# Hybrid encoder trunk on one core: gate projections woven apart from their branches, C's keys moved ahead of B's queries, and the last two feature tiles taken one by one

## The chip, the cores and the metric

The kernel runs on one core of one Trainium2 chip. Time is device time in microseconds (us) of that core. The core has TensorE (matrix products, PE in the profile, with its weight loads as PEld), VectorE (DVE), ScalarE (ACT), GpSimd (POOL) and SyncE (SP), which issues most transfers.

## The reference

An encoder of two layers (DEPTH = 2) works on 272 tokens: 16 learned meta tokens and 256 tokens on a grid of 4 rows by 64 columns, each with 1024 features. A layer is

```
h = h + 1/2 * SwiGLU1(RMSNorm(h))
n = RMSNorm(h)
h = h + ( sum_b sigmoid(gate_b(n)) * (mixer_b(n) @ w_branch[b]) ) @ w_out
h = h + 1/2 * SwiGLU2(RMSNorm(h))
```

SwiGLU goes through 2816 features. The three mixers b are attentions with 8 query heads of 64 features, fed by one projection of n: A has 2 key heads, a window of 128 positions, rotary positions and a sink logit for each head; B has 8 key heads, a neighbourhood of 4 rows by 16 columns and a learned bias; C has 2 key heads, is dense, and normalises each head of q and k before its rotary positions. The gates are 3 x 1024 columns of the same projection. After the last layer comes RMSNorm of all tokens, and the meta tokens are dropped. All data are float32.

## The kernel before, in words

**Layout.** The features of h stand on the partitions, eight tiles of 128 features by 272 tokens (256 where the meta tokens are no longer needed, in layer 1 from the queries on). A product in full precision is made of three products of rounded parts: `unit` (L218) loads a block of weights, 128 x 1024, into `raw`, casts it into `hi` on ScalarE (L250) and subtracts for `lo` on VectorE (L251), in the mixer for every third plain unit on GpSimd (`lo_engine`, L213). There are four buffers each of raw, hi and lo. `mm` (L284) goes over the feature tiles k and for each over two output tiles m, three matmuls each (L295 to L297). A projection of 256 columns is two units and 48 matmuls; a branch product has half of that.

**Order.** The program is written as a sequence, and a scheduler of the framework orders each engine's instructions ahead of time, by dependences, free buffers and the place in the program as priority. So the program's order sets preferences; what an engine then runs is a fixed queue. Accumulators (`acc`) have two buffers, score and transpose banks (`s`) three.

**The mixer (L724).** First come B's values and keys, four projections, around the norm's reciprocal root (`finish`, L351, with `rsqrt`, L313), then B's two query projections, evacuated by L773. Then three attentions run as generators. Each does its work for two query blocks times two halves of the heads: `products` (scores on TensorE, softmax on VectorE and ScalarE, normalisation in L439), then a `yield`, then transposes and value products of that step behind the next step's scores. With meta queries (layer 0) A and C have one more yield. At each yield `weave` (L914) takes one piece of a list of other work:

- during B: A's keys, C's keys (`c_keys`, L839), A's queries in two halves
- during A: C's queries in two halves (`c_queries`, L857), and then `gated(1, mp)`, mp = 0 to 3, which is B's output: a gate projection (evacuation L901, tanh L902), the branch product, and its combination with the gate (L907)
- during C: what is left of these, then `gated(0, mp)` for A
- behind C: `gated(2, mp)`, then the product with w_out

`c_keys` has a projection, squares, two sums over heads on TensorE, a reciprocal root of 272 columns on VectorE and ScalarE, rotary positions (`rope_c`, L826) and a split into stacked parts (`stack_k`, L471).

**Small operations.** `rsqrt` refines the root with L319, a scalar operation `-0.5 x + 1.5`. `grouped` (L504) negates A's sinks (L510) and copies them into another order for every half (L527). `v_prep` (L482) repeats the meta values (L485), B repeats its own (L647), the meta queries are copied into place (L565, L870), C's root is scaled in (L883) and out (L885), all on VectorE.

**The end.** `residual` (L299) adds a product of `ffn` to two feature tiles at once (L304) and hands them to the next norm. `Final` (L935) squares each pair (L942), multiplies it by the gain (L946), and transposes four tiles at a time (L955). `finish` (L960) sums the squares over features on TensorE (L965), takes the root (L968 and `rsqrt`), scales both halves (L972, L973) and stores them (L974).

## Time and profile before

| | us |
|---|---|
| median of 3 runs | 1339.12 |
| lowest and highest | 1338.96, 1340.93 |
| the profiled execution, whole | 1339.12 |
| the profiled execution, span of its instructions | 1337.3 |
| TensorE busy | 1308.9 |
| VectorE busy | 903.7 |
| ScalarE busy | 671.4 |
| GpSimd busy | 170.4 |

The page of a profile gives each engine's busy time, the groups of instructions by line, and the chain of work that ended last. A view of stretches gives, for a window a:b of the span in us, the window's length and then for each engine busy time and instruction count, the granted clock of TensorE, the busy share of the transfers and their GB/s. In a list of instructions in time a line begins with the start and the length in us, then engine, line of the program, operation, output<-inputs and the shape; in square brackets stands how long the engine was idle before and who ended that. In the view of one line, a row gives least/median/greatest length in ns and the first and last start. A view of waits gives who waited for whom: total, times, longest. Matmuls are pipelined and their ends are modelled. The granted clock was 0.996 of full over the profiled execution.

### The profile page before, as it was taken

What the parts mean: (1) busy time and instruction counts of PE and PEld (TensorE: products, weight loads), DVE (VectorE), ACT (ScalarE), POOL (GpSimd) and SP (SyncE); (2) the same over time, 40 slices, a digit from 0 to 9 for tenths busy, and PEclk for the clock granted to TensorE, in tenths of its full rate; (3) what the DMA queues carried; (4) which work ended last, traced back from release to release, by engine and by line L of the source; (5) the groups of instructions that cost most, each with busy time, mean ns of one, the idle gap of its engine ahead of it and who ended that gap; (6) DMA issues with size and microseconds to landing.
All of it is one profiled execution on the core that took longest, in us unless ns stands there. A gap on an engine that the chain in (4) does not pass through costs nothing. (4 is left out here: it accounts for less than half of the span.)

```text
span 1337.3 us, 26009 instructions
## 1 busy us (share of the span) xinstructions
PE 1308.9 (98%) x10683; PEld 1285.8 (96%) x10683; DVE 903.7 (68%) x1352; ACT 671.4 (50%) x1009; POOL 170.4 (13%) x115
## 2 busy tenths in 40 slices
PE   9999999988999999999999999999989999999997
PEld 8999999978999999999999999999889999999997
DVE  6655668699664587646676646677897567765663
ACT  6443444476554455434455434454776545543444
POOL 1000001332122220000000000022422233000000
PEclk9999999999999999999999999999999999999998
DMA  7765555532343676555565555555324456666652
GB/s 232 210 186 174 175 177 181 152 98 93 111 142 111 185 192 189 183 174 174 162 185 174 174 177 179 158 181 158 95 96 128 141 174 188 186 187 187 187 172 78
DMA packets 239010, 217.52 MB, mean 163 GB/s; under 512 B 24804, under 2 KB 237980, under 8 KB 238764
## 3 DMA queue, kind: packets, MB, share of 16 engines
q1 hardware_dynamic: 238540, 215.20, 53.1%
q8 instruction: 84, 1.38, 0.4%
q10 hardware_dynamic: 352, 0.66, 0.1%
q14 instruction: 34, 0.28, 0.1%
HBM read 214.78 MB, written 1.05 MB: 161 GB/s over the span
## 5 line engine op out<-in xcount | busy, mean ns | idle before, releaser
L250 ACT CAST hi<-raw 128x1024 fp32r<-128x1024 f32 (+1 forms) x386 | 398.6, 1033 | 551.6 <-PE acc L296 374.9
L296 PE MATMUL acc<-xl,hi 128*128 128x272 f32 (+1 forms) x2160 | 620.8, 287 | 0.0
L297 PE MATMUL acc<-xh,lo 128*128 128x272 f32 (+1 forms) x2160 | 619.2, 287 | 0.6 <-DVE lo L251 0.6
L295 PE MATMUL acc<-xh,hi 128*128 128x272 f32 (+1 forms) x2160 | 618.2, 286 | 0.6 <-DVE qk L766 0.6
L251 DVE TENSOR_TENSOR lo<-raw,hi 128x1024 fp32r<-128x1024 f32 (+1 forms) x349 | 424.1, 1216 | 215.3 <-ACT hi L250 213.0
L295 PEld LDWEIGHTS acc<-xh,hi 128*128 128x128 f32 x2160 | 408.1, 189 | 3.1 <-issue 2.7
L297 PEld LDWEIGHTS acc<-xh,lo 128*128 128x128 f32 x2160 | 406.8, 188 | 1.5 <-DVE lo L251 0.8
L296 PEld LDWEIGHTS acc<-xl,hi 128*128 128x128 f32 x2160 | 406.5, 188 | 1.1 <-issue 0.7
L296 PE MATMUL acc<-hl,hi 128*128 128x272 f32 (+1 forms) x704 | 201.9, 287 | 0.0
L297 PE MATMUL acc<-hh,lo 128*128 128x272 f32 (+1 forms) x704 | 201.1, 286 | 0.0
L295 PE MATMUL acc<-hh,hi 128*128 128x272 f32 (+1 forms) x704 | 200.4, 285 | 0.0
L295 PEld LDWEIGHTS acc<-hh,hi 128*128 128x128 f32 x704 | 132.7, 189 | 0.1
L297 PEld LDWEIGHTS acc<-hh,lo 128*128 128x128 f32 x704 | 132.3, 188 | 0.0
L296 PEld LDWEIGHTS acc<-hl,hi 128*128 128x128 f32 x704 | 132.2, 188 | 0.0
L251 POOL TENSOR_TENSOR lo<-raw,hi 128x1024 fp32r<-128x1024 f32 x37 | 91.6, 2475 | 229.2 <-ACT hi L250 217.4
L349 POOL TENSOR_TENSOR ss<-ss,scr 128x544 f32<-128x544 f32 (+1 forms) x12 | 17.4, 1448 | 602.2 <-ACT scr L346 602.1
L295 PE MATMUL acc<-oh,hi 128*128 128x272 f32 (+1 forms) x192 | 54.7, 285 | 0.0
L296 PE MATMUL acc<-ol,hi 128*128 128x272 f32 (+1 forms) x192 | 54.7, 285 | 0.0
L297 PE MATMUL acc<-oh,lo 128*128 128x272 f32 (+1 forms) x192 | 54.5, 284 | 0.0
L401 DVE TENSOR_TENSOR scr<-acc,scr 128x544 f32<-128x544 f32 (+1 forms) x40 | 28.6, 716 | 31.0 <-PE acc L297 30.9
L304 DVE SCALAR_TENSOR_TENSOR h<-acc,h 128x544 f32<-128x544 f32 (+1 forms) x40 | 28.5, 714 | 28.4 <-PE acc L297 28.3
L398 DVE TENSOR_TENSOR scr<-acc,rstd 128x544 f32<-128x544 f32 (+1 forms) x40 | 28.6, 716 | 26.2 <-PE acc L297 26.2
(257 smaller groups left out, 1367.1 us busy)
## 6 DMA issues: line engine op xcount, KB each, us to landing
raw<-in_ffn_w_in_dram SPq DMA_DIRECT2D x176, 512.0 KB, 3.6
raw<-in_ffn_w_out_dram SPq DMA_DIRECT2D x80, 512.0 KB, 3.4
raw<-in_w_in_dram SPq DMA_DIRECT2D x80, 512.0 KB, 3.8
raw<-in_w_in_dram SPq DMA_DIRECT2D x32, 256.0 KB, 3.2
raw<-in_w_branch_dram SPq DMA_DIRECT2D x32, 256.0 KB, 4.0
raw<-in_w_out_dram SPq DMA_DIRECT2D x16, 512.0 KB, 3.8
raw<-in_ffn_w_out_dram SPq DMA_DIRECT2D x16, 256.0 KB, 2.7
raw<-in_w_branch_dram SPq DMA_DIRECT2D x8, 512.0 KB, 3.4
```

Of the source, the lines that this page charges most:

```text
L250: ACT.copy(hi[:, :n], raw[:, :n])
L251: lo_engine().tensor_tensor(lo[:, :n], raw[:, :n], hi[:, :n].bitcast(F32), op=ALU.subtract)
L295: PE.matmul(o, a, rh, start=k == 0, stop=False)
L296: PE.matmul(o, a, rl, start=False, stop=False)
L297: PE.matmul(o, b, rh, start=False, stop=k == len(rows) - 1)
L304: DVE.scalar_tensor_tensor(hv, a[:, :, :n], 0.5, hv, op0=ALU.mult, op1=ALU.add)
L349: (DVE if j == 3 else POOL).tensor_tensor(ss, ss, dst, op=ALU.add)
L398: DVE.tensor_tensor(g, gate, rb, op=ALU.mult)
L401: DVE.tensor_tensor(g, up, g, op=ALU.mult)
```

## The change

**The weave.** `gated` is cut into `gate(b, mp)`, the projection with its tanh, and `branch(b, mp)`, the rest. A plan says for each yield which pieces are emitted. B's first two gates come during B and right behind it, B's branches and its other gates during A, A's gates and branches during C, and two of C's gates at C's end.

**C's keys** are emitted between B's keys and B's queries, and no longer during B's attention.

**Small operations.** Constants stand in a tile `cc`. Scalar operations on VectorE with two constants become operations that read a constant from `cc`, C's scaling is one operation instead of two, the sinks are reordered and negated once for both layers, and copies of the meta parts go from VectorE to ScalarE.

**The end.** In the last block of the last feed-forward part the two output tiles are computed one after the other. Tile 6 is added, squared, summed, multiplied and transposed by itself, and the table of the square root is asked for there by a root of a constant; then tile 7 follows, and `finish` only takes the root and scales.

```diff
+    cc = const.tile([128, 4], F32, name="cc")
+    for i, v in enumerate((1.5, HD * EPS, -1.0)):
+        POOL.memset(cc[:, i:i + 1], v)
...
-    def mm(acc, units, xh, xl, xk, n):
+    def mm(acc, units, xh, xl, xk, n, tiles=(0, 1)):
...
-            for m in range(2):
+            for m in tiles:
...
         a = acc_tile()
+        if isinstance(nxt, Final) and mp == 3:
+            for m in range(2):
+                mm(a, units, xh, xl, 0, n, (m,))
+                hv = h[:, 6 + m, :n]
+                DVE.scalar_tensor_tensor(hv, a[:, m, :n], 0.5, hv, op0=ALU.mult, op1=ALU.add)
+                nxt.tile(6 + m, n)
+            return
...
-        DVE.tensor_scalar(tmp, tmp, -0.5, 1.5, op0=ALU.mult, op1=ALU.add)
+        DVE.scalar_tensor_tensor(tmp, tmp, -0.5, cc[:, :1].to_broadcast(list(tmp.shape)), op0=ALU.mult, op1=ALU.add)
...
-            DVE.tensor_scalar(mx[:, i:i + 1], mx[:, i:i + 1], scale, -1.0, op0=ALU.mult, op1=ALU.mult)
+            DVE.scalar_tensor_tensor(mx[:, i:i + 1], mx[:, i:i + 1], scale, cc[:, 2:3], op0=ALU.mult, op1=ALU.mult)
...
-        DVE.tensor_copy(vrep, vt[:, None, GRID:].to_broadcast([128, 8, META]))
+        ACT.copy(vrep, vt[:, None, GRID:].to_broadcast([128, 8, META]))
...
-                    DVE.tensor_copy(qm[:, g, g, half * 32:half * 32 + 32].rearrange("p (t j) -> p t j", t=2),
-                                    q[half][:, g, :, GRID:])
+                    ACT.copy(qm[:, g, g, half * 32:half * 32 + 32].rearrange("p (t j) -> p t j", t=2),
+                             q[half][:, g, :, GRID:])
...
+            for i in range(DEPTH):
+                DVE.tensor_copy(sinks_tg[:, 0, 8 * i:8 * i + 8].rearrange("p (t g) -> p t g", g=2),
+                                sink[:, i, :].rearrange("p (g t) -> p t g", g=2))
+            DVE.tensor_scalar(sinks_tg[:, 1], sinks_tg[:, 0], -1.0, None, op0=ALU.mult)
...
-                DVE.tensor_scalar(rqv[:, :nq], rqv[:, :nq], 1.0 / HD, EPS, op0=ALU.mult, op1=ALU.add)
+                DVE.tensor_tensor(rqv[:, :nq], rqv[:, :nq], cc[:, 1:2].to_broadcast([128, nq]), op=ALU.add)
                 rsqrt(rq[:, :nq], rqv[:, :nq], t24[:, :nq])
-                DVE.tensor_scalar(rq[:, :nq], rq[:, :nq], 0.125, None, op0=ALU.mult)
...
+        c_keys()
+        qb = q_tile()
+        for half in range(2):
+            a = proj(plain(w, 0, 8, B_Q + half * 256), n_out)
...
-        others = [a_keys, c_keys, lambda: a_queries(0), lambda: a_queries(1)]
-        weave(neighbourhood(biases, qb, kb, vb, oh, ol, not last), others)
-        others += [lambda: c_queries(0), lambda: c_queries(1)]
-        others += [lambda mp=mp: gated(1, mp) for mp in range(4)]
-        weave(mix_a(), others)
-        others += [lambda mp=mp: gated(0, mp) for mp in range(4)]
-        weave(mix_c(), others)
-        others += [lambda mp=mp: gated(2, mp) for mp in range(4)]
-        for work in others:
-            work()
+        weave(neighbourhood(biases, qb, kb, vb, oh, ol, not last),
+              [[(a_keys,)], [(a_queries, 0)], [(gate, 1, 0)], [(a_queries, 1)], [(gate, 1, 1)]])
+        weave(mix_a(),
+              [[(branch, 1, 0), (c_queries, 0)], [(branch, 1, 1), (gate, 1, 2)], [(c_queries, 1)],
+               [(branch, 1, 2), (gate, 1, 3)], [(branch, 1, 3)]])
+        weave(mix_c(), [[(gate, 0, mp), (branch, 0, mp)] for mp in range(4)] + [[(gate, 2, 0), (gate, 2, 1)]])
+        for mp in range(4):
+            if mp > 1:
+                gate(2, mp)
+            branch(2, mp)
...
+        def tile(self, k, n):
+            if k == 6:
+                self.sq = scr()
+            ACT.activation(self.sq[:, k - 6, :n], h[:, k, :n], AF.Square)
+            if k == 6:
+                v = small()
+                ACT.activation(v[:, :1], ones[:, :1], AF.Sqrt)
+                self.pt = [bank("s", 3) for _ in range(2)]
+                self.st = [bank("s", 3), bank("pv")]
+            parts = [self.ss[:, 0], self.ss[:, 1], self.sq[:, 0]] if k == 6 else [self.sq[:, 1]]
+            for qi in range(2):
+                for i, part in enumerate(parts):
+                    PE.matmul(self.st[qi][:, :1], part[:, qi * 128:(qi + 1) * 128], ones[:, :1],
+                              start=k == 6 and i == 0, stop=k == 7)
+            self.gained(k, n)
+            for qi in range(2):
+                self.turn(self.pt[qi], qi, (4, 5, 6) if k == 6 else (7,))
```

`gained` is the multiplication by the gain (one tile), and `turn` makes the transposes of the tiles named.

More of the change, by code (lines that the diff above doesn't have):

```diff
@@ L767, in mixer @@
                                       bc(r[:, GRID:], 2), op=ALU.mult)
-        for half in range(2):
-            a = proj(plain(w, 0, 8, B_Q + half * 256), n_out)
-            for qi in range(2):
-                o = qb[:, 2 * half:2 * half + 2, qi * 128:(qi + 1) * 128]
-                back = bass.AP(tensor=o.tensor, offset=o.offset + 127, ap=[list(o.ap[0]), list(o.ap[1]), [-1, 128]])
-                DVE.tensor_tensor(back, a[:, :, qi * 128:(qi + 1) * 128], bc(r[:, qi * 128:(qi + 1) * 128], 2),
-                                  op=ALU.mult)
-            if not last:
-                DVE.tensor_tensor(qb[:, 2 * half:2 * half + 2, GRID:], a[:, :, GRID:T], bc(r[:, GRID:], 2),
-                                  op=ALU.mult)
         tab = None
@@ L869, in c_queries @@
             if not last:
-                DVE.tensor_copy(sqm[:, 2 * half:2 * half + 2, :], sq[:, :, GRID:])
+                ACT.copy(sqm[:, 2 * half:2 * half + 2, :], sq[:, :, GRID:])
                 if half:
@@ L882, in c_queries, with gate, branch @@
                 nq = 16 if last else 17
[L883 removed]
+                DVE.tensor_tensor(rqv[:, :nq], rqv[:, :nq], cc[:, 1:2].to_broadcast([128, nq]), op=ALU.add)
                 rsqrt(rq[:, :nq], rqv[:, :nq], t24[:, :nq])
[L885 removed]
         def mix_c():
             return grouped(2, qc, kc[0], vc, oh, ol, None, None, None, None, rq, not last)
[L891 to L893 removed]
+        c_keys()
[3 more added lines that the diff above has]
+            for qi in range(2):
+                o = qb[:, 2 * half:2 * half + 2, qi * 128:(qi + 1) * 128]
+                back = bass.AP(tensor=o.tensor, offset=o.offset + 127, ap=[list(o.ap[0]), list(o.ap[1]), [-1, 128]])
+                DVE.tensor_tensor(back, a[:, :, qi * 128:(qi + 1) * 128], bc(r[:, qi * 128:(qi + 1) * 128], 2),
+                                  op=ALU.mult)
+            if not last:
+                DVE.tensor_tensor(qb[:, 2 * half:2 * half + 2, GRID:], a[:, :, GRID:T], bc(r[:, GRID:], 2),
+                                  op=ALU.mult)
+        tot, halves = [], []
+        gates = {}
+        def gate(b, mp):
+            g = gates[b, mp] = sb.tile([128, 2, T], F32, name=nm("gate"), tag="gate", bufs=2)[:, :, :n_out]
+            a = proj(plain(w, 0, 8, GATES + b * D + mp * 256), n_out)
+            DVE.tensor_tensor(g, a[:, :, :n_out], rb[:, :, :n_out], op=ALU.mult)
+            ACT.activation(g, g, AF.Tanh, scale=0.5)
+        def branch(b, mp):
             if b == 1:
@@ L898, in gated @@
                 halves.extend([qk(4, T, dt=F32R) for _ in range(2)] for _ in range(2))
-            g = sb.tile([128, 2, T], F32, name=nm("gate"), tag="gate", bufs=2)[:, :, :n_out]
-            a = proj(plain(w, 0, 8, GATES + b * D + mp * 256), n_out)
-            DVE.tensor_tensor(g, a[:, :, :n_out], rb[:, :, :n_out], op=ALU.mult)
-            ACT.activation(g, g, AF.Tanh, scale=0.5)
+            g = gates.pop((b, mp))
             a = acc_tile()
@@ L945, in pair @@
             for k in (2 * j, 2 * j + 1):
-                ACT.activation(h[:, k, :n], h[:, k, :n], AF.Copy, scale=gcol[:, 48 + k:49 + k])
-            if j % 2:
-                self.half(j // 2)
-        def half(self, j):
-            self.pt = []
-            for qi in range(2):
-                pt = bank("s", 3)
-                for k in range(4):
-                    PE.transpose(pt[:, k * 128:(k + 1) * 128], h[:, 4 * j + k, qi * 128:(qi + 1) * 128], ident)
-                self.pt.append(pt)
-                if j == 0:
-                    evac(self.y[qi][:, :512], pt)
+                self.gained(k, n)
@@ L960, in finish @@
         def finish(self):
             dst = out[0].rearrange("(r q c) d -> q c r d", r=ROWS, q=2)
-            st = bank("s", 3)
+            v, r, t = small(), small(), small()
             for qi in range(2):
-                for i in range(4):
-                    PE.matmul(st[:, qi:qi + 1], (self.ss, self.sq)[i // 2][:, i % 2, qi * 128:(qi + 1) * 128],
-                              ones[:, :1], start=i == 0, stop=i == 3)
-            v, r, t = small(), small(), small()
-            DVE.tensor_scalar(v[:, :2], st[:, :2], 1.0 / D, EPS, op0=ALU.mult, op1=ALU.add)
+                DVE.tensor_scalar(v[:, qi:qi + 1], self.st[qi][:, :1], 1.0 / D, EPS, op0=ALU.mult, op1=ALU.add)
```

49 lines of the change are left out of this document (30 added, 19 removed).

## The prediction

> **What bounds the kernel now.** I read the page's first part and its groups, then the busy time by stretch, then who waits for whom, then single instructions in time.
>
> ```profile
> PE 1308.9 (98%) x10683; PEld 1285.8 (96%) x10683; DVE 903.7 (68%) x1352; ACT 671.4 (50%) x1009; POOL 170.4 (13%) x115
> ...
> L251 DVE TENSOR_TENSOR lo<-raw,hi 128x1024 fp32r<-128x1024 f32 (+1 forms) x349 | 424.1, 1216 | 215.3 <-ACT hi L250 213.0
> ```
>
> TensorE is busy for 98% of 1337.3 us: 28.4 us idle, and nothing here shortens its work. So the question is only where those idle microseconds lie. The stretches tell (share of each engine, then granted clock; 40:60 is a feed-forward stretch for comparison):
>
> ```profile
> 40.00:60.00 20.00, 20.00 (x163) 20.00 (x162) 12.74 (x14) 8.97 (x10) 0.00 (x0) 1.00 0.79 205
> 240.00:260.00 20.00, 19.89 (x168) 18.70 (x167) 11.08 (x35) 9.72 (x26) 5.63 (x7) 1.00 0.50 144
> 260.00:340.00 80.00, 70.98 (x582) 64.78 (x582) 74.73 (x184) 56.60 (x135) 24.55 (x18) 1.00 0.30 93
> 340.00:440.00 100.00, 98.11 (x824) 94.63 (x823) 61.00 (x115) 50.16 (x90) 25.36 (x13) 1.00 0.44 127
> 900.00:920.00 20.00, 19.36 (x160) 19.17 (x159) 14.92 (x35) 7.58 (x15) 7.57 (x7) 1.00 0.56 168
> 920.00:1000.00 80.00, 73.70 (x604) 67.89 (x605) 68.95 (x172) 57.13 (x137) 26.13 (x20) 0.98 0.33 100
> 1000.00:1100.00 100.00, 100.00 (x897) 98.11 (x892) 63.56 (x115) 54.91 (x97) 26.70 (x13) 1.00 0.49 147
> ```
>
> The feed-forward stretch loses nothing and runs 163 matmuls in 20 us, 0.123 us each. The loss is in the two mixers, in the part with branch B and the front of branch A: 9.02 of 80 us in layer 0 (11.3%), 6.30 of 80 in layer 1 (7.9%). VectorE has 74.73 us of work there, more than TensorE's 70.98 (ratio 1.05; layer 1: 68.95 to 73.70, 0.94). Later, with gate projections between the steps, the ratio is 61.00 to 98.11 (0.62) and the loss 1.9%; in layer 1 it is 0.64 and 0%. Matmul ends are modelled and cover short holes, so I keep the weight loads as a second measure: idle 15.22 us (19.0%) against 5.4% in layer 0, 12.11 us (15.1%) against 1.9% in layer 1. Between 260 and 340 the longest waits name VectorE:
>
> ```profile
> PE s L541 <- DVE sm L419: 3.6, 2, 2.0
> PE s L684 <- DVE sm L419: 2.3, 2, 1.9
> ```
>
> **The weave.** A gate projection needs only the norm, so it can fill holes anywhere in the mixer; before, there is none in the lossy part of layer 0 until its very end:
>
> ```profile
> L901 DVE TENSOR_TENSOR gate<-acc,rstd x24: 681/701/725, 329.1 to 1113.7; 128x544 f32<-128x544 f32 x12, 128x512 f32<-128x512 f32 x12
> ```
>
> One gate is 48 matmuls, 48 x 0.123 = 5.9 us of TensorE; its branch is 24, 2.9 us; together 8.8. On VectorE the pair has three weight splits of 1.216 us, a third of which go to GpSimd (2.4 us), and two full-size operations of 0.70, 3.9 us. So a pair brings VectorE and TensorE in the ratio 0.44, which thins the VectorE-bound part out.
>
> The other half is what leaves it. C's keys go ahead of B's query projections. Their VectorE work:
>
> ```profile
> 275.12 1.85 DVE L316 RECIPROCAL scr<-scr 128x272 f32<-128x272 f32 x1 [0.98 <-ACT scr L315]
> 277.89 0.41 DVE L318 TENSOR_TENSOR scr<-scr 128x272 f32<-128x272 f32 x1
> 283.10 1.47 DVE L854 TENSOR_TENSOR scr<-scr,scr 128x272 f32<-128x272 f32 x1
> 285.80 1.77 DVE L479 TENSOR_TENSOR qk<-scr,qk 64x272 fp32r<-64x272 f32 x4
> ```
>
> 1.85 + 1.47 + 1.77, ten other operations of this size at about 0.41 like L318 (4.1), and one of two splits (1.2) make 10.4 us; TensorE 5.9 us. Of the moved small operations the trace has:
>
> ```profile
> L485 DVE COPY vrep<-v x4: 212/218/219, 267.5 to 975.8; 128x128 f32<-128x128 f32 x4
> L565 DVE CAST qm<-qk x8: 151/172/173, 293.2 to 349.4; 128x32 fp32r<-128x32 f32 x8
> L527 DVE COPY sm<-sink x8: 96/164/723, 304.0 to 1005.6; 128x4 f32<-128x4 f32 x8
> L647 DVE COPY vrb<-qk x1: 415/415/415, 231.8 to 231.8; 128x512 f32<-128x512 f32 x1
> ```
>
> Layer 0: 8 x 0.17, 4 x 0.16, 2 x 0.22, 0.42 and four or five like L527 make 3.5 us off VectorE; layer 1, without the meta queries, 1.4. What ScalarE takes over it has room for (56.60 of 80). The sink copies made once wait at the mixer's start for a transfer, with VectorE's bias work queued behind; a microsecond or two there, under projections, at nothing.
>
> Now the sum, by a straight line through the measured pairs of ratio and loss. Layer 0: the lossy part holds after the change 70.98 - 5.9 + 3 x 8.8 = 91.5 us of TensorE work (the first of branch B's four pairs was already in it) and 74.73 - 10.4 - 3.5 + 3 x 3.9 = 72.5 of VectorE: ratio 0.79. Between (0.62, 1.9%) and (1.05, 11.3%) that is 5.6%, 5.4 us; the same work lost 9.02 + 0.5 before. Gain 4.1 us. Layer 1: 73.70 - 5.9 + 4 x 8.8 = 103.0 and 68.95 - 10.4 - 1.4 + 4 x 3.9 = 72.8, ratio 0.71, loss 1.9%, 2.0 us instead of 6.30. Gain 4.3. By the weight loads the same line gives 10.5 us instead of 16.7, and 5.3 instead of 12.8: gains 6.2 and 7.5. So the part gains 8.4 to 13.7 us.
>
> C's keys cost something where they go. There VectorE had 11.08 of 20 us (14.92 in layer 1); with 10.4 more over 26 us the ratios are 0.82 and 1.00, the losses 1.7 and 2.7 us instead of 0.11 and 0.64: 3.7 us back. The cover of this move is B's two query projections, 11.8 us of TensorE; the queries of B come out 5.9 us later, and B's scores wait for them. Net 4.7 to 10.0 us; neither measure is the better one, so I take the middle, 7.4 us gained.
>
> Two activation-table loads go as well. Before, C's keys need a square root in the middle of B's exponentials:
>
> ```profile
> 273.36 1.28 ACT L315 ACT_TABLE_LOAD   x1
> ...
> 275.93 1.28 ACT L421 ACT_TABLE_LOAD   x1
> ```
>
> After, it stands behind the norm's own square root, before any exponential. That is 2.6 us of ScalarE in each layer, beside a busier VectorE; I count it in the line above, not again.
>
> **The swapped operations.** Scalar operations become ones that read a constant tile, and this can speak against the change. In the root of the norms:
>
> ```profile
> L319 DVE TENSOR_SCALAR scr<-scr x8: 293/296/302, 29.8 to 1151.7; 128x272 f32<-128x272 f32 x7, 128x256 f32<-128x256 f32 x1
> L318 DVE TENSOR_TENSOR scr<-scr x8: 411/438/443, 29.4 to 1151.3; 128x272 f32<-128x272 f32 x7, 128x256 f32<-128x256 f32 x1
> ```
>
> With two tensors to read, the eight full-width L319 should cost 0.14 us more each, 1.1 us in all, off TensorE's path while two accumulators wait; I take 0, bound 1.1. The Trainium skill, "VectorE: DVE Perf Modes", section "Mode 2×_2P", says the same: a scalar operation in SBUF uses both read ports for one tensor and runs at double rate, a two-tensor operation cannot; by it the swap costs those 1.1 us, and the rows agree. What the swap may be for is this:
>
> ```profile
> 324.06 2.34 DVE L883 TENSOR_SCALAR rqv<-rqv 128x17 f32<-128x17 f32 x1
> ...
> 323.59 2.78 POOL L251 TENSOR_TENSOR lo<-raw,hi 128x1024 fp32r<-128x1024 f32 x1 [3.47 <-ACT hi L250]
> ...
> 307.06 3.44 DVE L439 TENSOR_TENSOR p<-p,sm 128x1024 f32<-128x1024 f32 x1
> ...
> 307.04 2.37 POOL L251 TENSOR_TENSOR lo<-raw,hi 128x1024 fp32r<-128x1024 f32 x1 [8.73 <-ACT hi L250]
> ```
>
> A 17-element scalar operation takes 2.34 us because it ends with GpSimd's split, so VectorE waits out GpSimd. But the two-tensor L439 does so too. The swap therefore frees nothing; value 0. The Trainium skill, "SBUF — State Buffer", section "Who interferes with whom", has the rule that an operation with two SBUF inputs is blocked as well while GpSimd reads; the trace agrees, and by it the sum stays as it is.
>
> **The tail.** Now the last two feature tiles:
>
> ```profile
> 1326.25 0.28 PE L297 MATMUL acc<-hh,lo 128*128 128x256 f32 x1
> 1326.37 0.60 PE L955 MATMUL s<-cst,h 128*128 128x128 f32 x4
> 1328.44 0.58 PE L965 MATMUL s<-ones,ss 128*128 128x1 f32 x4
> 1328.89 0.58 PE L965 MATMUL s<-ones,scr 128*128 128x1 f32 x4
> ...
> 1326.57 0.69 DVE L304 SCALAR_TENSOR_TENSOR h<-acc,h 128x512 f32<-128x512 f32 x1 [6.32 <-PE acc L297]
> 1327.29 0.63 ACT L942 ACTIVATE scr<-h 128x512 f32<-128x512 f32 x1 [5.44 <-DVE h L304]
> 1327.95 0.91 ACT L946 ACTIVATE h<-h,gcol 128x256 f32<-128x256 f32 x2
> 1328.88 1.28 ACT L315 ACT_TABLE_LOAD   x1
> 1330.17 0.20 ACT L315 ACTIVATE sm<-sm 128x2 f32<-128x2 f32 x1
> 1331.40 0.88 DVE L972 TENSOR_SCALAR p<-p,sm 128x512 f32<-128x512 f32 x2
> ```
>
> From the last matmul's start to L972 are 5.15 us; scaling, stores and their landing behind it stay. After the change: 0.32 to VectorE, a 256-wide residual of about 0.42 (L773, quoted below, is that wide), a square of about 0.45 (half of L946's pair), sums of the last tile 0.6, two VectorE operations, and 0.05 to the square root, whose table is already there: 2.1 us; then 1.23 as now: 3.33. So 1.8 us shorter. But work that stood behind the last matmul now stands before it: six sums of two passes and six transposes, 18 passes. L965 has 8 passes in 0.90 us, 0.11 each: 2.0 us in TensorE's order, with no idle time there to take them. Net +0.2. Bounds: -1.8 if they are fitted behind, +1.5 if tile 6's transposes wait for the 1.28 us table load, which now stands before their input on ScalarE, and hold the last matmuls back. All three units of weights of the last block are needed after 3.5 us instead of 7; I price that at 0, as in the trace splits run ahead by more.
>
> **Sum.** 1339.1 (the profiled execution; 1.8 us of it lie outside the span; it equals the median) - 7.4 + 0.2 = 1331.9 us. About 2.7 us, 0.2%, is what a measurement tells from no change.
>
> **The rivals.**
> Full recovery: the lossy part runs at the later part's pace, and C's keys cost nothing. For it: the ratio falls below TensorE's everywhere. Against: score, exponential, normalisation and transpose stay a chain of four engines. By the two measures 14.0 to 22.3 us, middle 18: 1321.
> VectorE stays the bound: its order, not its sum, decides; the queue keeps its lumps of 2 to 3 us behind GpSimd (3.44 above), and B's part gets gates which bring 1.2 us splits of their own. Then perhaps a third of the net 7.4 us: 1337.
> Slower: C's keys in one lump. If their 10.4 us run on VectorE ahead of the evacuation of B's queries, two splits (2.4) and the evacuations behind them, with the latencies of a square, a root and two passes over TensorE, it is 16 to 18 us against 11.8 of cover: TensorE idle for about 5 in each layer. It decides if the weave gains under 10 besides; with half of the 8.4 gained it gives 1339 + 10 - 4 = 1345. For it: VectorE runs its queue in order. Against: it had 8.9 us idle in 240:260.
> The change doesn't do what it says: the issue order is a scheduler's, and the program's order only a wish:
>
> ```profile
> 239.32 0.90 ACT L236 CAST hi<-raw 128x128 fp32r<-128x128 f32 x4 [1.99 <-PE acc L296]
> ...
> L773 DVE TENSOR_TENSOR qk<-acc,rstd x8: 411/420/425, 242.4 to 922.7; 128x256 f32<-128x256 f32 x8
> ```
>
> The first casts of A's keys start at 239.32 us, before the first evacuation of B's queries at 242.4, though written behind both. If the scheduler arrived at one order from either text: 1339.
>
> **How the numbers follow.** Forecast 0.55 (own range 1327 to 1336), full recovery 0.17, VectorE-bound 0.15, slower 0.08, no effect 0.05. The range 1320 to 1338 takes in full recovery's middle and the VectorE-bound case; left out are the slower case, no effect and the far end of full recovery. Faster: 0.55 + 0.17 + half of 0.15, 0.80. Same: the other half and 0.05, 0.12. Slower: 0.08.
>
> **What would show it.** Right: gate operations from about 265 us on; VectorE's share between 260 and 340 down to about 0.75; one table load instead of three between 240 and 300 us; the idle time of TensorE in each mixer down by 2 to 5 us; TensorE's last matmul preceded by sums and transposes, and 3.3 us from it to the scaling. Wrong: waits of TensorE on the evacuation of B's queries, or VectorE still above 0.9 there.

## The result and the profile after

The changed kernel takes 1351.40 us (median of 4 runs, 1348.77 to 1356.13), the kernel before in the same session 1339.07 us (4 runs, 1338.96 to 1340.93). The ratio is 1.0093, 95% interval 1.0078 to 1.0108: slower by 12 us. The forecast was 1331.9, and the range ended at 1338.

The profiled execution was the slowest of the four, 1356.13 us, with a span of 1354.3. Line numbers have moved: L250 and L251 are now L255 and L256, L425 is L438, L426 is L439, L541 is L550, L518 is L530, L907/L909 are L927/L929. First the first part of the page, then the busy time by stretch, for the stretches that the prediction used.

```profile
PE 1318.1 (97%) x10683; PEld 1294.7 (96%) x10683; DVE 900.1 (66%) x1330; ACT 671.9 (50%) x1024; POOL 166.7 (12%) x118
```

```profile
240.00:260.00 20.00, 17.90 (x141) 17.21 (x141) 17.80 (x35) 12.06 (x31) 7.65 (x11) 0.98 0.47 142
260.00:340.00 80.00, 76.07 (x609) 70.97 (x609) 58.23 (x147) 48.52 (x124) 21.06 (x15) 0.96 0.36 111
340.00:440.00 100.00, 95.08 (x814) 90.85 (x814) 62.30 (x130) 54.69 (x108) 25.25 (x14) 1.00 0.42 116
920.00:1000.00 80.00, 75.55 (x615) 70.48 (x614) 58.69 (x139) 48.99 (x123) 29.11 (x24) 0.96 0.41 126
1000.00:1100.00 100.00, 91.77 (x792) 88.39 (x791) 71.31 (x137) 59.02 (x114) 24.21 (x13) 0.97 0.39 113
```

TensorE has the same 10683 matmuls. Its idle time went from 1337.3 - 1308.9 = 28.4 to 1354.3 - 1318.1 = 36.2 us, and its busy time rose by 9.2 us. The target of the weave did get better: idle in 260:340 fell from 9.02 to 3.93 us, in 920:1000 from 6.30 to 4.45, and VectorE's share there from 0.93 and 0.86 to 0.73 and 0.73. But 1000:1100, which lost nothing before, now loses 8.23 us, 340:440 loses 4.92 instead of 1.89, and 240:260 loses 2.10 instead of 0.11. Who TensorE waited for (total, times, longest):

```profile
PE s L530 <- ACT p L439: 4.6, 7, 1.6
PE s L650 <- ACT vk L135: 3.9, 2, 2.5
PE s L550 <- ACT p L439: 3.5, 3, 1.6
...
PE pv L621 <- ACT pts L135: 1.5, 1, 1.5
```

L439 is C's exponential. It needs the scale of L438, the line that changed from a scalar operation to one that reads a constant from `cc`. The view of one line for it, before and after (least/median/greatest ns):

```profile
L425 DVE TENSOR_SCALAR sm<-sm,rq x33: 192/207/216, 364.3 to 1054.6; 128x1 f32<-128x1 f32 x33
```

```profile
L438 DVE SCALAR_TENSOR_TENSOR sm<-sm,rq,cc x33: 198/219/2398, 373.3 to 1085.7; 128x1 f32<-128x1 f32 x33
```

The median is nearly the same, the longest is eleven times as long, for one element on each partition. The list in time shows what the long ones share: before, with GpSimd at work, and after.

```profile
1052.11 1.29 POOL L909 TENSOR_TENSOR tot<-tot,gate 128x512 f32<-128x512 f32 x1 [11.33 <-DVE gate L907]
1052.64 0.33 DVE L425 TENSOR_SCALAR sm<-sm,rq 128x1 f32<-128x1 f32 x2
...
1053.35 2.38 POOL L251 TENSOR_TENSOR lo<-raw,hi 128x1024 fp32r<-128x1024 f32 x1
1053.36 0.22 DVE L425 TENSOR_SCALAR sm<-sm,rq 128x1 f32<-128x1 f32 x1
```

```profile
1050.95 2.37 POOL L256 TENSOR_TENSOR lo<-raw,hi 128x1024 fp32r<-128x1024 f32 x1 [8.01 <-ACT hi L255]
1051.39 3.18 DVE L438 SCALAR_TENSOR_TENSOR sm<-sm,rq,cc 128x1 f32<-128x1 f32 x2
1053.28 1.27 POOL L929 TENSOR_TENSOR tot<-tot,gate 128x512 f32<-128x512 f32 x1
...
1063.57 1.29 POOL L929 TENSOR_TENSOR tot<-tot,gate 128x512 f32<-128x512 f32 x1 [9.02 <-DVE gate L927]
...
1064.10 3.09 DVE L438 SCALAR_TENSOR_TENSOR sm<-sm,rq,cc 128x1 f32<-128x1 f32 x2
1064.80 2.37 POOL L256 TENSOR_TENSOR lo<-raw,hi 128x1024 fp32r<-128x1024 f32 x1
```

Before, two scale operations run in 0.33 us in the middle of GpSimd's sum, and one in 0.22 us under its split. After, the pair that starts at 1051.39 ends at 1054.57; GpSimd's two instructions end at 1053.32 and 1054.55. The pair at 1064.10 ends at 1067.19, GpSimd's second instruction at 1067.17. In all, ten of the 33 operations of L438 take over 0.7 us, and each of the ten ends within 0.02 us of an instruction of GpSimd. Before, 15 of the 33 of L425 began under an instruction of GpSimd, and none took over 0.22 us.

The rise of TensorE's busy time is in the granted clock. Short stretches around the start of branch B and the end of C in layer 0 (the granted clock stands behind POOL's entry):

```profile
256.00:258.00 2.00, 0.76 (x7) 0.51 (x5) 1.71 (x4) 2.00 (x7) 1.79 (x3) 1.00 0.22 78
258.00:260.00 2.00, 1.14 (x7) 0.88 (x8) 2.00 (x7) 1.98 (x5) 1.36 (x2) 0.84 0.30 88
260.00:262.00 2.00, 2.00 (x19) 1.38 (x19) 1.19 (x3) 0.54 (x1) 0.00 (x0) 0.50 0.63 182
...
438.00:440.00 2.00, 0.70 (x7) 0.57 (x8) 0.54 (x2) 1.24 (x3) 1.44 (x1) 1.00 0.75 243
440.00:442.00 2.00, 1.70 (x10) 1.44 (x11) 0.23 (x1) 0.21 (x1) 0.90 (x1) 0.57 0.08 27
```

TensorE is busy for 1.90 of 4 us and then runs at half clock; after 0.70 of 2 us it does so again. Ahead of the kernel's end this execution has five such stretches, of 6.83, 6.83, 6.83, 3.41 and 3.41 us (from 259.4, 440.3, 938.6, 1068.3 and 1085.4 us), 27.3 us in all. At half clock up to half of that time is lost, 13.7 us; before, there was one stretch of 3.41 us at 960.8, up to 1.7. The difference of 12.0 is an upper bound, since TensorE waits in such stretches too; it covers the 9.2 by which busy time rose. It holds for this execution alone: its mean granted clock was 0.988, that of the other three runs 0.992 to 0.994, that of the profiled execution before 0.996. By these clocks the half clock makes an estimated 3 to 5 of the 12 us between the medians, and idle time the rest. The prediction said nothing about the clock.

### The profile page after: what moved, and what is told of

It reads as the page before. It is cut to its first block, busy times and chain, and to the rows that moved or that the text cites. A ratio compares the mean times of both kernels' runs of the same rounds, so it can differ in the third digit from the quotient of the medians.

```text
span 1354.3 us, 25990 instructions
## 1 busy us (share of the span) xinstructions
PE 1318.1 (97%) x10683; PEld 1294.7 (96%) x10683; DVE 900.1 (66%) x1330; ACT 671.9 (50%) x1024; POOL 166.7 (12%) x118
## 5 line engine op out<-in xcount | busy, mean ns | idle before, releaser
L255 ACT CAST hi<-raw 128x1024 fp32r<-128x1024 f32 (+1 forms) x386 | 398.1, 1033 | 549.9 <-PE acc L301 374.2
L256 DVE TENSOR_TENSOR lo<-raw,hi 128x1024 fp32r<-128x1024 f32 (+1 forms) x349 | 421.9, 1210 | 217.9 <-ACT hi L255 214.9
L256 POOL TENSOR_TENSOR lo<-raw,hi 128x1024 fp32r<-128x1024 f32 x37 | 89.7, 2425 | 271.2 <-ACT hi L255 249.2
L317 DVE SCALAR_TENSOR_TENSOR h<-acc,h 128x544 f32<-128x544 f32 (+1 forms) x39 | 27.8, 714 | 22.1 <-PE acc L302 22.0
```

What stands on the lines that cost most here:

```text
L255: ACT.copy(hi[:, :n], raw[:, :n])
L256: lo_engine().tensor_tensor(lo[:, :n], raw[:, :n], hi[:, :n].bitcast(F32), op=ALU.subtract)
L317: DVE.scalar_tensor_tensor(hv, a[:, :, :n], 0.5, hv, op0=ALU.mult, op1=ALU.add)
```

## The experiments

**The theory** was that one line, L438, carries the loss, because an operation with two inputs in SBUF waits out GpSimd's instructions, and that the half clock follows the thin stretches that such waits make. **The rivals** were the new order itself (C's keys in one lump, the gates at C's end), the new end, and the form of the operation without GpSimd. Ratios are to the kernel before, run on the same chip, with their 95% intervals; where two other kernels are compared, it is by their medians.

**The three parts by themselves.** Each of these is the kernel before with one part of the change, as the diff ahead of the prediction has it; here a line of each. The small operations:

```diff
-            DVE.tensor_scalar(mx[:, i:i + 1], mx[:, i:i + 1], scale, -1.0, op0=ALU.mult, op1=ALU.mult)
+            DVE.scalar_tensor_tensor(mx[:, i:i + 1], mx[:, i:i + 1], scale, cc[:, 2:3], op0=ALU.mult, op1=ALU.mult)
...
-        DVE.tensor_copy(vrep, vt[:, None, GRID:].to_broadcast([128, 8, META]))
+        ACT.copy(vrep, vt[:, None, GRID:].to_broadcast([128, 8, META]))
```

> The kernel before with the small operations of the change alone (weave and end as before). Theory 1: the negated scale of C's scores (L425 before, L438 after), which now reads two tensors in SBUF, waits out GpSimd's work, and the scores wait for it; it hurts with the old weave too, which also has GpSimd splits during C: 1342 to 1348 us, some L425 instances over 0.7 us. Rival 2 (the weave itself is what hurts, by uncovering B's start and C's end): 1337 to 1340 us.

The weave and the move of C's keys:

```diff
+        c_keys()
+        qb = q_tile()
...
-        others = [a_keys, c_keys, lambda: a_queries(0), lambda: a_queries(1)]
-        weave(neighbourhood(biases, qb, kb, vb, oh, ol, not last), others)
+        weave(neighbourhood(biases, qb, kb, vb, oh, ol, not last),
+              [[(a_keys,)], [(a_queries, 0)], [(gate, 1, 0)], [(a_queries, 1)], [(gate, 1, 1)]])
```

> The kernel before with the weave alone (gates apart from branches, C's keys ahead of B's queries). Theory 1: layer 1's C part runs without holes, but B's start (258 and 938 us after) and C's end in layer 0 (438 us) stay uncovered, each followed by a stretch at half clock: 1338 to 1344 us. Rival 2: all of the loss is here, 1347 to 1352 us. The prediction's own reading (VectorE relieved): 1330 to 1334 us.

The end:

```diff
+        if isinstance(nxt, Final) and mp == 3:
+            for m in range(2):
+                mm(a, units, xh, xl, 0, n, (m,))
...
+                nxt.tile(6 + m, n)
```

> The kernel before with the end alone (last two feature tiles one by one). Both theories: the root of a constant is issued hundreds of us too early and only adds table loads, the last load stays at the end; 18 passes go ahead of the last matmul: 1339.5 to 1342 us. If the prediction's sum of the end holds: 1337.5 to 1340.5 us.

The small operations: 1344.74 us, 1.0039 [1.0026, 1.0052]. The weave with the move of C's keys: 1338.69, 0.9989 [0.9979, 0.9999]. The end: 1340.55, 1.0011 [1.0002, 1.0021]. All three lie in the range of their first theory. By the ratios the operations cost 5.2 us, the weave gains only 1.5, and the end costs as much. The three add up to +5.2, and together they cost 12: the parts act on each other.

**The line.** First the changed kernel with the old form of this one line, then the kernel before with its new form alone.

```diff
-            DVE.scalar_tensor_tensor(mx[:, i:i + 1], mx[:, i:i + 1], scale, cc[:, 2:3], op0=ALU.mult, op1=ALU.mult)
+            DVE.tensor_scalar(mx[:, i:i + 1], mx[:, i:i + 1], scale, -1.0, op0=ALU.mult, op1=ALU.mult)
```

> The changed kernel with one line as before: the negated scale of C's scores is again a scalar operation with a constant. Theory 1: the waits of up to 2.4 us in that line go, and with them layer 1's two stretches at half clock between 1060 and 1090 us: 1341 to 1345 us. Rival 2: 1349 to 1352 us, no change.

> The kernel before with one line changed: the negated scale of C's scores reads the constant from a tile. Theory 1: this line makes the whole loss of the small operations alone (1344.7 us): 1343 to 1346 us. Rival (another of the small operations does it): 1338.5 to 1340.5 us.

The changed kernel without it: 1338.01 us, 0.999 [0.998, 0.9999]. The kernel before with it: 1347.21, 1.0053 [1.0038, 1.0068]. By the medians one line costs 13.4 us in the changed kernel and 7.5 in the old one, in both more than was expected. Alone it costs more than all the small operations together, so the others give something back; which of them was not taken apart. In the old kernel the row of the new line is nearly the same as in the changed one:

```profile
L429 DVE SCALAR_TENSOR_TENSOR sm<-sm,rq,cc x33: 198/219/2394, 364.7 to 1061.5; 128x1 f32<-128x1 f32 x33
```

No stretch of half clock lies in the mixers of that execution (1.00 in all its windows there); TensorE is idle for 1344.5 - 1308.7 = 35.8 us, 7.4 more than before. Six of the 33 take over 0.7 us, and what they take beyond the median adds up to the same 7.4 us. So here the line's price is idle time alone; in the changed kernel the half clock comes on top.

**The order.** With the line put back, what does the new order still lose? C's keys back into B's attention; C's first gates behind C's end.

```diff
-        c_keys()
         qb = q_tile()
...
-              [[(a_keys,)], [(a_queries, 0)], [(gate, 1, 0)], [(a_queries, 1)], [(gate, 1, 1)]])
+              [[(a_keys,)], [(c_keys,)], [(a_queries, 0), (gate, 1, 0)], [(a_queries, 1)], [(gate, 1, 1)]])
```

```diff
-        weave(mix_c(), [[(gate, 0, mp), (branch, 0, mp)] for mp in range(4)] + [[(gate, 2, 0), (gate, 2, 1)]])
+        weave(mix_c(), [[(gate, 0, mp), (branch, 0, mp)] for mp in range(4)])
         for mp in range(4):
-            if mp > 1:
-                gate(2, mp)
+            gate(2, mp)
```

> The changed kernel with the scale line as before (1338.0 us) and C's keys back among B's attention, at the second yield. Theory 1: the hole at B's start (VectorE solid from 244 to 260 us, waits of 3.5 us in all on the copies of B's values, half clock behind it) is the lump of C's keys; it goes, but two table loads and 10 us of VectorE come back into B's attention, so about even: 1335 to 1340 us, idle time of TensorE in 240:280 below 2.5 us instead of 4.0. Rival: the hole comes from the queries of A being cast ahead of the copies, and stays: 1338 to 1343 us with the wait on the copies of B's values still over 2 us.

> The changed kernel with the scale line as before (1338.0 us) and all gates of C behind C's end, as the kernel before had them. Theory 1: in layer 0 the last gates were emitted ahead of the meta queries' tail and leave it without cover (2.6 us idle in 400:440 and a stretch at half clock); with them behind it 1334.5 to 1337 us, nothing changes in layer 1. Rival: the tail of C is as long as any gate cannot cover, because the fixed queue of TensorE puts it first: 1337 to 1339 us.

C's keys back: 1341.38, 1.0014 [1.0005, 1.0023], slower than without that edit and above the 1335 to 1340 of the theory. The hole at B's start closes (38.88 of 40 us busy in 240:280, against 36.03), but another opens in B:

```profile
PE s L693 <- DVE sm L432: 7.5, 3, 4.7
```

C's gates behind: 1337.05, 0.998 [0.9969, 0.9991]; TensorE in 400:440 went from 37.39 to 39.23 us busy, and the half clock there is gone, and so is the wait of L621 that is listed above. With two gates in the queue ahead of the tail of C's meta queries, nothing was left to cover that tail. In the total the gain of 1.0 us is not clear of the noise.

Then the best parts together: the small operations without the scale line, weave, C's gates behind C's end, the old end. And C's keys moved further up, ahead of B's keys.

> The scale line as before, C's gates behind C's end, and the end of the kernel before (two tiles at once). Theory 1: the new end costs about 1.1 us, as it does alone, so 1334.5 to 1337 us against 1337.05; the spread of several us between runs stays, with the granted clock, since B's start still has its hole. Rival (the new end is worth something once the mixer is right): 1337 to 1339 us.

> As the kernel with the old end, but C's keys stand ahead of B's keys, two projections earlier. Theory 1: the hole at B's start (waits of 3.9 us on the copies of B's values, 4.5 us idle in 240:280, half clock behind it in both layers) comes of VectorE's and ScalarE's work for C's keys meeting that for B's queries and A's keys; with 11.8 us more between, idle time in 240:280 falls below 2 us, the half-clock stretches at B's start go and the time is 1329 to 1334 us, with a spread under 3 us. Rival (the hole is the order of casts ahead of the copies, whatever stands before): 1335 to 1338 us, waits on the copies as before.

```diff
-        for dst, c0 in ((vb, B_V), (kb, B_K)):
-            in_mixer[0] = dst is kb
+        def keys_or_values(dst, c0, a):
...
+        keys_or_values(vb, B_V, a)
...
         c_keys()
+        keys_or_values(kb, B_K, None)
```

1336.26, 0.9969 [0.9958, 0.9979], and 1336.37, 0.9976 [0.9967, 0.9984]. The first is as expected; the second misses its 1329 to 1334. It moved the hole and did not close it: the wait of 3.4 us for the copies of B's values became

```profile
PE acc L300 <- DVE qk L769: 4.9, 3, 2.1
```

**The end.** The changed kernel asks for the square root's table with a root of a constant. That activation depends on nothing, so the scheduler put it 260 us ahead, into C's exponentials, and the load comes again at the end:

```profile
1086.05 1.28 ACT L992 ACT_TABLE_LOAD   x1
1087.35 0.20 ACT L992 ACTIVATE sm<-ones 128x1 f32<-128x1 f32 x1
1087.57 1.28 ACT L439 ACT_TABLE_LOAD   x1
...
1345.78 1.28 ACT L328 ACT_TABLE_LOAD   x1
```

```diff
-                ACT.activation(v[:, :1], ones[:, :1], AF.Sqrt)
+                ACT.activation(v[:, :1], self.sq[:, 0, :1], AF.Sqrt)
```

> The changed kernel with the scale line as before (1338.0 us) and the early root taken of tile 6's squares instead of a constant, so that it cannot be issued before them. Theory 1: its table load moves from C's softmax in layer 1 (1068.6 us) to tile 6, the load at the end (1.28 us, 1.0 of it waited for) goes, and two loads in the mixer: 1336 to 1337.3 us. Rival: tile 6's transposes wait for the load in ScalarE's queue and hold TensorE's last matmuls for over 1 us: 1337.5 to 1339.5 us.

From the residual of the third pair (L304, now L317) to the scaling (L972, now L1012) the kernel before takes 1331.40 - 1319.55 = 11.85 us, the changed one 1348.30 - 1335.33 = 12.97. With the root tied to tile 6's squares:

```profile
1321.92 0.69 DVE L317 SCALAR_TENSOR_TENSOR h<-acc,h 128x512 f32<-128x512 f32 x1 [0.17 <-PE acc L302]
...
1333.93 0.88 DVE L1012 TENSOR_SCALAR p<-p,sm 128x512 f32<-128x512 f32 x2
```

That is 12.01, and the load lies at 1326.35, in tile 7's matmuls. The whole took 1339.02, 0.9995 [0.9984, 1.0005], beside 0.999 without this edit: the 1 us cannot be seen in the total, whose runs lie 5.5 us apart. That total lies in the rival's range, but what the rival describes did not happen: tile 6's last transposes run behind the load at 1329.36, among tile 7's matmuls, which follow each other without a gap up to the last one at 1330.63. From that one to the scaling are 3.30 us, where the prediction had 3.33.

**The clock.** The runs of these kernels spread, 1332.7 to 1338.2 in the one with the best parts, and time goes with the mean clock: 0.996 in the runs of 1332.70, 1332.74 and 1333.15, 0.992 in those of 1337.97 and 1338.24. To test what makes the clock fall, useless matmuls were put into the hole at B's start. They compute nothing that is used.

```diff
+                if qi and kt:
+                    fill = bank("pv")
+                    for _ in range(8):
+                        PE.matmul(fill[:, :128], ident, kb[:, 0, 0, :128], start=True, stop=True)
```

> The kernel of the run before last but one (small operations without the scaled line, weave, C's gates behind C's end, the old end), with 8 matmuls of 128 by 128 added per mixer at the start of B's attention, where TensorE waits 3.4 us for the copies of B's values; they compute nothing that is used. Theory (the half clock follows a thin stretch of TensorE): the stretches of half clock at about 259 and 932 us are gone, the wait stays covered by useless work, and the median is 1332 to 1334.5 us, with a spread of the runs under 3 us. Rival (the clock drops for another reason than the idle stretch ahead of it): the stretches stay, and the median is 1336 to 1338.5 us.

> The same with 4 useless matmuls per mixer instead of 8. Theory (the half clock follows a thin stretch of TensorE): between the kernel without them (1336.3 us) and the one with 8, some of the runs with the half clock at the start of B and some without. Rival (another reason): 1336 to 1338 us with the half clock as before.

With 8: 1334.68, 0.9966 [0.9952, 0.998], 1334.46 to 1336.38, 0.2 us above the range that was expected, and the clock of the five runs is 0.995 to 0.998. Short stretches at B's start in both layers, without the fill and with it:

```profile
254.00:258.00 4.00, 2.57 (x23) 2.32 (x22) 3.67 (x10) 3.92 (x12) 2.02 (x3) 1.00 0.42 131
258.00:262.00 4.00, 3.33 (x28) 2.42 (x28) 2.96 (x8) 2.28 (x4) 1.12 (x2) 0.65 0.48 135
926.00:930.00 4.00, 2.36 (x22) 2.10 (x20) 3.95 (x10) 3.15 (x9) 0.82 (x2) 1.00 0.43 131
930.00:934.00 4.00, 3.62 (x17) 2.45 (x17) 2.67 (x9) 3.66 (x9) 1.21 (x2) 0.71 0.44 131
```

```profile
254.00:258.00 4.00, 4.00 (x35) 4.00 (x35) 3.96 (x10) 2.16 (x6) 0.27 (x2) 1.00 0.65 216
258.00:262.00 4.00, 3.48 (x35) 3.05 (x33) 3.71 (x11) 3.98 (x10) 3.15 (x4) 1.00 0.24 73
926.00:930.00 4.00, 4.00 (x37) 3.86 (x35) 3.91 (x10) 2.80 (x8) 0.82 (x2) 1.00 0.35 116
930.00:934.00 4.00, 2.98 (x16) 1.94 (x15) 3.71 (x13) 3.92 (x11) 1.56 (x2) 1.00 0.44 124
```

The fill alone keeps the clock up, so the thin stretch is what lowers it. In time it only pays for itself: the ratio is that of the kernel without it. With 4, half the fill, the half clock came back in layer 1 (0.83 in 920:940), at B's start in layer 0 the clock stayed at 1.00, and the time was 1337.83, 0.9988 [0.9979, 0.9997], with clocks from 0.992 to 0.997: not between the other two times, as the theory had it, but in the rival's range.

All traces together say more precisely what a thin stretch is. In the changed kernel the five stretches start at 259.4, 440.3, 938.6, 1068.3 and 1085.4 us, and these times lie 53, 146, 38 and 5 times 3.413 us apart: the clock changes on a grid of steps of 3.41 us. In the five steps just ahead, TensorE is busy for 1.43, 1.87, 0.90, 1.44 and 1.51 us. Take all steps at full clock between 20 and 1200 us in the 19 traces: each of the 23 with less than 1.69 us of work was followed by half clock, of the next 38, up to 2.29 us, it was 7, and of the 6464 with more it was 3. Busy time is modelled, so the border may be sharper than this. Where the grid falls on a hole may be what differs from run to run; that was not tested.

**GpSimd taken away.** So far the wait for GpSimd was argued from ends that coincide. This kernel is the old one with the new line, and all splits, sums and products that GpSimd does in the mixers given to VectorE:

```diff
-        return POOL if in_mixer[0] and unit_no[0] % 3 == 0 else DVE
+        return DVE
...
-                    (DVE if g else POOL).tensor_tensor(l_, r_, h_.bitcast(F32), op=ALU.subtract)
+                    DVE.tensor_tensor(l_, r_, h_.bitcast(F32), op=ALU.subtract)
...
-                POOL.tensor_tensor(tt, tt, g, op=ALU.add)
+                DVE.tensor_tensor(tt, tt, g, op=ALU.add)
```

and likewise for the split of paired heads and for a sum and a product of the rotary positions.

> The kernel before with only the line of C's exponent scale changed, as in the run that isolated it, and besides every weight split, sum and product of GpSimd in the mixers moved to VectorE, so that GpSimd works on nothing there but fills of constants. Theory (the two-input form waits for GpSimd's instruction to end): all 33 instructions of the line take 198 to 230 ns, where the isolating run had 33 at 198/219/2394 ns; the busy time of the group falls from 13.9 to about 7.2 us. Rival (the form is slow in itself now and then, or waits for something else, such as a transfer or ScalarE): some of the 33 still take over 1000 ns. The total says nothing here, since VectorE gets about 60 us of work more: 1345 to 1365 us by both.

```profile
L429 DVE SCALAR_TENSOR_TENSOR sm<-sm,rq,cc x33: 198/213/221, 360.8 to 1047.4; 128x1 f32<-128x1 f32 x33
```

The line is short in all 33, with the same form: what it waited for was GpSimd. But the total was 1331.22 us (one run), below the kernel before, where both theories had expected 1345 to 1365. So the same edit was made alone, in the changed kernel, and in the version with the best parts, with and without the fill. GpSimd is called still where it has this work no more.

> The kernel before with GpSimd's splits, sums and products of the mixers moved to VectorE and nothing else. Theory (every VectorE operation with two SBUF inputs waits out GpSimd's instructions, and these waits cost more than GpSimd saves): 1329.5 to 1333 us, and the form of the scale line is worth under 0.5 us once GpSimd is still. Rival (GpSimd hurts only the scale line, which has one input here): VectorE has some 60 us more to do in the mixers, 1339 to 1347 us.

> The changed kernel, its scale line with two inputs included, with GpSimd's work of the mixers on VectorE. Theory (the scale line's wait for GpSimd carries the loss of the change): the 33 instructions take under 230 ns and the median is 1327 to 1334 us, 17 to 24 under the changed kernel. Rival (the loss comes from elsewhere: the new order, or the form itself): not under 1342 us.

> The best version of the change's parts so far (small operations without the scale line, weave, C's gates behind C's end, the old end; 1336.3 us) with GpSimd's work of the mixers on VectorE. Theory (weave and a still GpSimd fill the same holes of TensorE): 1326 to 1331 us, 0 to 5 under the kernel before with a still GpSimd. Rival (they add up): 1336.3 - 7.7 = 1328.6 us or less, with the kernel before at 1331. Second rival (with 60 us more on VectorE the gates in B's part are in its way): 1332 us and over.

> The same with the 8 useless matmuls at B's start. Theory (half clock follows a thin stretch): 1.0 to 2.5 us under the same without them, and no half clock at the start of B. Rival: the hole at B's start is another without GpSimd's work, so that they only cost: 0 to 3.5 us more.

| | GpSimd works | GpSimd still |
|---|---|---|
| kernel before | 1339.07 | 1329.82, 0.9926 [0.9913, 0.9938] |
| changed kernel | 1351.40, 1.0093 [1.0078, 1.0108] | 1321.42, 0.9865 [0.985, 0.988] |
| best parts | 1336.26, 0.9969 [0.9958, 0.9979] | **1316.92**, 0.9828 [0.9815, 0.9841] |
| best parts and fill of 8 | 1334.68, 0.9966 [0.9952, 0.998] | 1320.92, 0.9859 [0.9845, 0.9872] |

With GpSimd still, the change that costs 12 us gains 8.4, and the best parts gain 12.9. The kernel before came out in its range; the changed kernel and the best parts came out below theirs (1327 to 1334, 1326 to 1331). Against the kernel before of the same session the best parts alone gave 3.6 us and the still GpSimd alone 10.5; together they give 23.4, more than the sum, and why was not taken apart. The fill costs 4.0, more than either side had; without it there is no half clock in the mixers, so this run does not test the clock. That the form of the line is worth under 0.5 us once GpSimd is still is not shown either: with it the kernel before took 1331.22 in its one run, without it 1329.82. For the changed kernel with GpSimd still, the row of the line and the stretches:

```profile
L438 DVE SCALAR_TENSOR_TENSOR sm<-sm,rq,cc x33: 197/214/221, 363.0 to 1052.6; 128x1 f32<-128x1 f32 x33
```

```profile
240.00:260.00 20.00, 20.00 (x173) 19.42 (x172) 17.65 (x42) 12.88 (x31) 0.00 (x0) 1.00 0.47 142
260.00:340.00 80.00, 80.00 (x674) 75.85 (x672) 67.84 (x177) 51.67 (x131) 0.00 (x0) 1.00 0.42 126
340.00:440.00 100.00, 97.97 (x826) 94.42 (x826) 71.96 (x142) 55.38 (x107) 0.72 (x3) 1.00 0.44 122
...
920.00:1000.00 80.00, 79.93 (x695) 75.61 (x694) 69.23 (x176) 53.73 (x128) 0.00 (x0) 1.00 0.44 133
1000.00:1100.00 100.00, 99.91 (x885) 97.84 (x883) 76.77 (x132) 60.77 (x102) 0.00 (x0) 1.00 0.52 148
```

TensorE loses nothing in B's part, with VectorE at 0.85 there, and runs at full clock in all these stretches. What is left in 340:440 is the tail of C's meta queries, which the best parts cover; they also have the shorter end (1.1 us). Those two make 3.1 of the 4.5 us between the two versions; the rest was not taken apart.

## Why the prediction was wrong

**The step that failed is "The swap therefore frees nothing; value 0".** The prediction worked from two lines of the swap, L319 and L883, and from L439 beside them, and bounded the cost by 1.1 us of duration. That size was about right for L319, whose eight full-width operations took 424/438/703 ns afterwards (L332). But the prediction has no word on L425, which stood in the same diff: 33 operations, 15 of them begun under GpSimd's instructions, none over 216 ns. Here nothing waited, so here the swap could lose something. Measured: 7.5 us alone, 13.4 with the other edits. That is 13.4 of the 19.5 us between the forecast and the result. Without the line the changed kernel is at 1338.01, still 6.1 above the forecast, and that part is taken up under the weave. The Trainium skill, "SBUF — State Buffer", section "Who interferes with whom", says in the same list that the prediction drew on that an operation of VectorE with at most one SBUF input, outside the modes that use both ports, does not contend with GpSimd. The trace agrees (0.33 us for two under a sum of GpSimd, 3.18 for two of the new form), and the rule was applied to L439, which has two inputs in both kernels, and not to the line that changed sides.

**Under it lies a reading that was wrong: VectorE as the limit of B's part.** The prediction took VectorE's 74.73 us of 80 for its own work, and fitted a line of loss against the ratio of loads. But part of that busy time is waiting inside the instruction. The kernel before with GpSimd still has this first line of its page, and these stretches in B's part:

```profile
PE 1310.5 (99%) x10683; PEld 1287.3 (97%) x10683; DVE 925.7 (70%) x1442; ACT 672.2 (51%) x1009; POOL 21.9 (2%) x25
...
260.00:340.00 80.00, 76.54 (x621) 70.83 (x622) 75.38 (x214) 59.92 (x144) 0.00 (x0) 0.98 0.32 97
920.00:1000.00 80.00, 77.84 (x640) 71.76 (x640) 73.53 (x207) 60.19 (x147) 0.00 (x0) 0.98 0.33 98
```

VectorE has ninety instructions more (1442 for 1352) and yet only 22 us more of busy time, 925.7 for 903.7, where the 37 plain splits alone bring 39.8 (the group of L251 went from 424.1 to 463.9 us). In B's part it is busier than before (75.38 and 73.53 us for 74.73 and 68.95), and still TensorE's idle time falls from 9.02 to 3.46 and from 6.30 to 2.16 us. At this ratio, 0.98 in layer 0, the prediction's line has a loss of about 10%; 4.3% were lost. Set against the median of the same line and shape with GpSimd still, the instructions that take over 0.1 us longer have an estimated excess of 11.8 in the 74.73 us and of 9.2 in the 68.95, and every one of them overlaps with an instruction of GpSimd. The products of the weights with the meta part, for one, before and with GpSimd still (busy, then mean ns):

```profile
L531 DVE TENSOR_TENSOR pm<-p,sm 128x64 f32<-128x64 f32 x16 | 9.0, 563 | 0.0
```

```profile
L531 DVE TENSOR_TENSOR pm<-p,sm 128x64 f32<-128x64 f32 x16 | 3.5, 218 | 0.0
```

In the mixers of the kernel before, TensorE waits for none of GpSimd's results; its longest wait, 2.0 us for the softmax step L419 at 313.1 us, comes behind the L439 of 3.44 us that the prediction shows. A ratio of loads cannot show that. That such waits make up all of the 10 us is not shown, because the same edit also made the splits shorter: 1.20 us each on VectorE, 2.48 on GpSimd. The prediction quoted L883 at 2.34 us and L439 at 3.44 beside GpSimd's split, and stopped at the remark that the swap does not help them.

**The weave** did in B's part what the prediction says, but less of it, and a term was missing. In the run with the weave alone, which gained 1.5 us, idle time in B's part fell by 4.63 and 2.35 us, where 8.4 to 13.7 in all were forecast. In 240:260 it rose by 1.87 us; 3.7 was the price set for both layers. And in 340:440 and 1000:1100, from which the gates were taken, it rose by 1.55 and 1.81 us: the prediction put this loss of cover at nothing. With GpSimd still the whole change gains 8.4 us, near the 7.2 predicted (7.4 less the end's 0.2); but the forecast was worked out for a kernel with GpSimd at work, so that this agrees is luck. Of what "would show it", the gates, VectorE's share (0.73 for a forecast of 0.75) and one table load instead of three between 240 and 300 us (L674, at 259.25) came out. Idle time fell by 5.1 and 1.9 us in B's part, but the mixers as a whole, for which 2 to 5 us each were forecast, did not gain.

**C's keys' new place** was priced at 3.7 us of queueing ahead of B's queries. The loss is where B starts: idle in 240:260 is up by 2.0 us. There TensorE waits for the copies of B's values on ScalarE (L135). In the list of ScalarE's instructions of the changed kernel these stand behind the stacking of C's keys (L490), for which ScalarE was idle 3.13 us until VectorE had finished the keys (L857), and behind casts for A's queries:

```profile
253.97 1.73 ACT L490 CAST qk<-scr 64x272 fp32r<-64x272 f32 x4 [3.13 <-DVE scr L857]
255.72 1.94 ACT L241 CAST hi<-raw 128x256 fp32r<-128x256 f32 x6
257.57 0.58 ACT L135 COPY vk<-s 88x512 f32<-88x512 f32 x1
```

Put back, the keys cost more (+3.4 us), so the slower rival, "C's keys in one lump", had the place nearly right but is not what made the kernel slow.

**The end**: +0.2 was predicted, with the table loaded early. The sum holds to the tenth where that is so (12.01 for 11.85). In the changed kernel it is not so; the hoisted load makes +1.1, and 2.56 us of table loads appear in C's exponentials.

**The clock** was missing from the sum. TensorE's 28.4 us of idle time was treated as what could be won or lost; in the profiled execution up to 12 us more came from half clock after thin stretches, in the other runs an estimated 3 to 5. The Trainium skill, "TensorE: Matmul & The Clock Gate", section "What's actually happening", has a window of 3413 ns and the half rate after an idle one. The lengths agree (3.41 and 6.83 us); but in these traces it took no idle window: 0.90 to 1.87 us of work in a step of 3.41 were little enough.

## What to carry to other kernels

Before swapping an operation for one with another input from SBUF, look at what GpSimd does at that moment, and at the greatest duration in its row, not the mean: an operation that never waited is the one that can start to. An engine's busy share can include waits inside its instructions, so an engine that looks full may be cured by taking work from its neighbour, even onto itself. When a gain does not come, look at the granted clock of the short stretches: holes of about 2 us were followed here by 3.41 or 6.83 us at half clock, which is up to 1.7 or 3.4 us of work.

## What the runs showed of the hardware

- An operation of VectorE on one element per partition, with one tensor from SBUF and a scalar for each partition, took 192 to 216 ns, and so did the 15 of 33 that began under GpSimd's instructions. With two tensors from SBUF it took up to 2398 ns, ending with GpSimd's instruction, and 197 to 221 ns without GpSimd's work.
- GpSimd's splits, sums and products in the mixers took 148 us (170.4 to 21.9 us busy). On VectorE, whose own waits then fell away, they raised its busy time by 22 us, and the kernel was 0.74% faster.
- TensorE's clock was halved for 3.41 or 6.83 us, on a grid of 3.41 us, after each step with less than 1.69 us of work, after some with up to 2.29 and after hardly any with more. It stayed at 1.00 where useless matmuls filled such steps. Runs of one kernel differed by 5.5 us with it.
- An activation that depends on nothing was moved 260 us ahead by the scheduler and cost two table loads of 1.28 us, each followed by its activation 0.01 to 0.02 us later.
